# Two transformer blocks in one kernel: reciprocal sums turned on TensorE, wide projection slices, early bias rows, gate beside up

## The chip, the cores and the metric

The kernel runs on one core of a Trainium2 chip. The metric is the device time of one execution in microseconds (us), as the median of several executions. Engines are named as the profile names them: PE (TensorE), PEld (its weight loads), DVE (VectorE), ACT (ScalarE), POOL (GpSimd), SP (SyncE, which issues most DMAs).

## The reference, cut to what matters

1024 tokens of width 1024 run through two blocks, all in float32. Only the parts that the change touches are shown.

```python
# block 1: one input projection, three attentions, then a feed-forward part
proj = rmsnorm(x, attn_pre_norm) @ w_in      # 512 q + 128 k + 128 v (window attention),
                                             # 768 + 4 (forget attention), 256 + 128 + 32 (latent attention)
bias = rel_bias[t5_causal_bucket(dist)]      # window attention: 32 buckets x 8 heads, over 256 keys per row
s = q @ k.T * 64**-0.5 + bias; s = where(in_band, s, -1e30)

# block 2: window attention over 8 blocks of 128 rows, 8 heads in 2 groups, one sink per head
p = softmax(concat([sink, s_ctx, s_loc]))    # 256 context keys, up to 384 local keys
out = p_ctx @ v_ctx + p_loc @ v_loc

# block 2: 16 experts, each takes its top 128 tokens
y = (silu(xs @ w_gate) * (xs @ w_up)) @ w_down * g   # all three weights 1024 x 1024 per expert
```

## The kernel before

Float32 products run as three matmuls each (`mm3`, lines 185 to 188: high x high, high x low, low x high) on operands that `split` (lines 169 to 171) has cut in a high part (ACT) and a low part (DVE). A planner orders each engine's instructions ahead of time from the program's order and its own estimate of readiness; the engines then run their lists in that order and wait on semaphores. SP's list is one such queue: a DMA issue that waits holds up those behind it.

**Opening of block 1.** `x_load` loads one of eight tiles of 128 tokens, normalizes it and transposes it on PE (`to_T`). `slice_mm` multiplies a tile with a slice of the token-major columns of the projection. These 804 columns are cut in four slices `SL` of 196, 204, 204 and 200 columns; the first runs inside the loop over `x`, the other three after `feat_proj`, from tiles `wht`, `wlt` of a pool of their own (`a2`). `feat_proj` (line 262) makes five groups of 128 columns the other way round, 512 tokens at a time. Between them the relative bias is made: one matmul (line 330) gives 8 rows of 384 values on 8 partitions, and one DMA (line 333) writes each of them 128 times to the DRAM tensor `toep_d`, from which `toep` is read back skewed (line 342) for the window attention.

**Attention of block 2.** Steps are counted by u = 8 t + h. `att_scores` makes one head's scores, their minimum on DVE (line 1128) and the exponential with its sum on ACT (line 1132). `att_pT` transposes four heads' probabilities of one key block on PE (line 1159) and copies them out on ACT or DVE; `att_pv` multiplies them with the values (line 1179). One step of `ATT` says which of these follow which scores. The product is accumulated transposed, in one PSUM tile `po` for a block t, and there is one such buffer (`PSO = 1`), so the next block's product begins when DVE has read `po` (line 1183). Each column of `po` is a query, so the reciprocal sums, which come as [query, head], are needed along the columns: line 1142 writes `rec` to DRAM, and line 1146 reads it back twice, spread over 64 partitions each. Meanwhile POOL scales and splits the output weights `wor`, which SP loads in the same queue.

**Experts.** For each of 16 experts and four groups of 256 hidden columns, `ex_gu` multiplies 128 gathered tokens with a gate tile and an up tile, each of 1 MB ([128, 8 x 256]), 48 matmuls of 256 columns into the two halves of `pg`; `ex_T` turns the result; `ex_down` multiplies it with a third tile of 1 MB, 12 matmuls of 512 columns. Weight tiles are fetched in the order of `order` into a ring of 17 buffers, and `wsplit` splits each in two pieces of 1024 columns (lines 1487, 1488). `x_T` transposes the next expert's tokens at the end of an expert.

Of the kernel before, what the change touches and what calls it, by code (L numbers as in the profile page):

```python
# [17 lines left out]
P = 128  # L18
S = 1024
# [73 lines left out]
def tile_two_blocks(ctx, tc, A, out):  # L93
# [50 lines left out]
    rec_d = [dram.tile([8, P], F32, name=f"rec_d{t}") for t in range(NT)]  # L144
# [78 lines left out]
    swa_pool = AP_(name="swa", bufs=1, side="left")  # L223
    qa = swa_pool.tile([P, 8, S], F32R, name="qa")
    kad = swa_pool.tile([P, 2, S], F32R, name="kad")
    kal = swa_pool.tile([P, 2, S], F32R, name="kal")
    va = swa_pool.tile([P, NT, P], F32, name="va")
# [32 lines left out]
    blank_lo(kal, 2)  # L260

    def feat_proj(f, done):
# [5 lines left out]
        for hf in range(2):  # L268
# [11 lines left out]
    def slice_w(pool, c0, w, nk=8):  # L280
        wh = pool.tile([P, 8, 204], F32R, name="wht", tag="wht")
        wl = pool.tile([P, 8, 204], F32R, name="wlt", tag="wlt")
        for k in range(0, 8, nk):
            raw = pool.tile([P, nk, 204], F32, name="rawt", tag="rawt", bufs=1)
            nc.sync.dma_start(raw[:, :, :w], A["w1t"].rearrange("p (k c) -> p k c", k=8)[:, k:k + nk, c0:c0 + w])
            split(wh[:, k:k + nk, :w], wl[:, k:k + nk, :w], raw[:, :, :w])
        return wh, wl

    def slice_mm(t, wh, wl, w, parts):
        ps = ps_o.tile([P, 512], F32, name="ps", tag="po")  # L290
        for k in range(8):
            mm3(ps[:, :w], hT_hi[:, k, trow(t)], hT_lo[:, k, trow(t)], wh[:, k, :w], wl[:, k, :w], k == 0, k == 7)
        for (dst, s0, s1, d0) in parts:
            nc.scalar.copy(dst[:, t, d0:d0 + s1 - s0], ps[:, s0:s1])

    with TP(name="a0", bufs=1, side="right") as a0:
        g1 = row_in(a0, "attn_pre_norm")
        swt = []

        def x_load(t, _):  # L300
# [11 lines left out]
        def x_mm(t, _):  # L312
            slice_mm(t, swt[0][0], swt[0][1], SL[0][1], SL[0][2])

# [7 lines left out]

    with TP(name="a5", bufs=1, side="right") as a5:
        rb = a5.tile([33, 8], F32, name="rb")
        nc.vector.memset(rb, -BIG)
        nc.sync.dma_start(rb[0:32, :], A["rel_bias"])
        oh = a5.tile([33, 384], F32, name="oh")
        nc.sync.dma_start(oh, A["onehot"])
        psB = ps_s.tile([P, 1024], F32, name="psB", tag="s")
        nc.tensor.matmul(psB[0:8, :384], rb, oh, start=True, stop=True)  # L330
        rowb = a5.tile([8, 384], F32, name="rowb")
# [8 lines left out]
    tp_pool = AP_(name="toep", bufs=1, side="right")  # L340
    toep = tp_pool.tile([P, 8, 256], F32, name="toep")
    nc.sync.dma_start(toep, toep_d[:, 127:127 + 383 * P].rearrange("h (p m) -> p h m", m=383)[:, :, 0:256])
# [762 lines left out]
    def att_scores(t, h, pb=None):  # L1105
# [28 lines left out]
        if h == 7:  # L1134
# [29 lines left out]
    def att_pv(g, c):  # L1164
# [10 lines left out]
        b = h // 4  # L1175
        for i in range(nk):
# [4 lines left out]
        if h + G == 8 and j == len(vt) - 1:  # L1181
            rb = atts[t][4]
            nc.vector.tensor_tensor(out=rb, in0=po, in1=rb, op=ALU.mult)
# [269 lines left out]
    for i in range(4 * NE + 2):  # L1453
        if i < 4 * NE:
            order += [("w_gate", i), ("w_up2", i)]
        if i >= 2:
            order.append(("w_down2", i - 2))
# [42 lines left out]
    with TP(name="sel", bufs=1, side="left") as sel, TP(name="selp", bufs=2, space=PSUM) as pst:  # L1500
# [22 lines left out]
        for wname, i in (("w_gate", 0), ("w_up2", 0)):  # L1523
# [81 lines left out]
    with TP(name="exg", bufs=2, space=PSUM) as psg, \  # L1605
# [40 lines left out]
        def ex_gu(i, _):  # L1646
# [16 lines left out]
            for gi, wname in enumerate(("w_gate", "w_up2")):  # L1663
# [212 lines left out]
```

## Time and profile before

| what | before |
|---|---|
| median of 3 executions | 2552.72 us (2550.89 to 2553.92) |
| the profiled execution | 2561.14 us, of which the span of its instructions is 2559.3 us |
| mean granted TensorE clock in it | 0.964 |
| PE busy | 2363.4 us, 92% of the span, 14750 matmuls |
| DVE, ACT, POOL busy | 63%, 44%, 22% |
| DMA | 384.04 MB, mean 150 GB/s |

A line of waits reads: engine, tile and line that waited, who released it, total us, times, longest. A line of the timeline reads: start, duration, engine, line, operation, out<-in, and in brackets the idle time before it and what ended it. Matmuls are pipelined: a matmul's cost in a stream is the distance between two starts, which is shorter than its duration.

### The profile page before, as it was taken

How to read it: one execution, taken by the hardware profiler on the slowest of the kernel's cores; microseconds unless marked ns; L12 is line 12 of the kernel's file. 1: busy time of each engine (PE TensorE's matmuls, PEld its weight loads, DVE VectorE, ACT ScalarE, POOL GpSimd, SP SyncE). 2: the span in 40 equal slices, each digit the busy share in tenths (PEclk: the TensorE clock that was granted, in tenths of full speed). 3: DMA queues.
4: the chain of work that ended last, by engine and by line, in shares of the span. 5: the costliest groups of instructions: out<-in, count | busy, mean ns of one | idle time of the engine just before them, and what ended most of it. 6: DMA issues, size and time to landing. Idle time of an engine off the chain costs nothing. (4 is left out here: it accounts for less than half of the span.)

```text
span 2559.3 us, 37811 instructions
## 1 busy us (share of the span) xinstructions
PE 2363.4 (92%) x14750; PEld 1982.4 (77%) x14750; DVE 1618.4 (63%) x2572; ACT 1116.0 (44%) x1940; POOL 570.6 (22%) x596
## 2 busy tenths in 40 slices
PE   7599999999999999999997999887958999999996
PEld 7497777787887878788877988554747999989885
DVE  4217557456677665444568733564377999988886
ACT  4217357443331222222224312432135778777775
POOL 1000252131000000000016200343053554464412
PEclk9799999999999999999999999889978999999998
DMA  4400103234243332111135110112787999999975
GB/s 142 91 21 31 51 18 96 79 115 141 95 148 108 116 99 66 41 50 50 52 89 149 59 50 13 33 43 81 256 299 291 370 373 383 384 362 347 352 253 206
DMA packets 126287, 384.04 MB, mean 150 GB/s; under 512 B 21183, under 2 KB 34432, under 8 KB 109724
## 3 DMA queue, kind: packets, MB, share of 16 engines
q1 hardware_dynamic: 114444, 347.54, 38.6%
q0 software_dynamic: 6048, 22.02, 3.7%
q10 hardware_dynamic: 5616, 12.06, 1.2%
q8 instruction: 116, 1.90, 0.3%
q14 instruction: 63, 0.52, 0.1%
HBM read 342.17 MB, written 39.40 MB: 149 GB/s over the span
## 5 line engine op out<-in xcount | busy, mean ns | idle before, releaser
L1488 DVE TENSOR_TENSOR wl<-raw,wh 128x1024 fp32r<-128x1024 f32 x378 | 469.6, 1274 | 58.7 <-ACT wh L1487 55.5
L1487 ACT CAST wh<-raw 128x1024 fp32r<-128x1024 f32 x382 | 392.5, 1050 | 89.3 <-PE pg L188 62.8
L186 PE MATMUL pg<-wh,xh 128*128 128x256 f32 x1024 | 295.3, 288 | 4.5 <-ACT xh L170 4.5
L187 PE MATMUL pg<-wl,xh 128*128 128x256 f32 x1024 | 294.5, 288 | 0.0
L188 PE MATMUL pg<-wh,xl 128*128 128x256 f32 x1024 | 293.0, 286 | 0.0
L186 PE MATMUL psu<-hT_hi,wh 128*128 128x512 f32 x704 | 278.7, 396 | 7.2 <-ACT wh L170 7.1
L170 ACT CAST wh<-raw 128x512 fp32r<-128x512 f32 (+1 forms) x177 | 107.4, 641 | 404.9 <-PE psu L187 230.4
L187 PE MATMUL psu<-hT_lo,wh 128*128 128x512 f32 x704 | 278.1, 395 | 0.0
L188 PE MATMUL psu<-hT_hi,wl 128*128 128x512 f32 x704 | 277.2, 395 | 0.2 <-DVE wl L171 0.2
L163 POOL TENSOR_TENSOR rrstd<-vrstd,neghalf 128x1 f32<-128x1 f32 x51 | 34.3, 700 | 849.5 <-DVE vrstd L160 849.4
L171 DVE TENSOR_TENSOR wl<-raw,wh 128x512 fp32r<-128x512 f32 (+1 forms) x177 | 124.6, 732 | 147.8 <-ACT wh L170 147.3
L869 DVE TENSOR_TENSOR ffn_y<-ffn_y,psd 128x512 f32<-128x512 f32 x160 | 108.6, 685 | 157.7 <-PE psd L188 157.1
L186 PEld LDWEIGHTS pg<-wh,xh 128*128 128x128 f32 x1024 | 198.2, 194 | 8.5 <-ACT xh L170 6.1
L188 PEld LDWEIGHTS pg<-wh,xl 128*128 128x128 f32 x1024 | 198.1, 193 | 3.2
L187 PEld LDWEIGHTS pg<-wl,xh 128*128 128x128 f32 x1024 | 198.2, 194 | 2.4 <-DVE wl L1488 0.3
L1621 POOL TENSOR_SCALAR hot<-iota,slot 128x128 bf16<-128x128 f32 x112 | 181.1, 1636 | 25.4 <-PE pi L1629 25.4
L186 PEld LDWEIGHTS psu<-hT_hi,wh 128*128 128x128 f32 x704 | 133.2, 189 | 39.4 <-ACT wh L170 9.4
L188 PEld LDWEIGHTS psu<-hT_hi,wl 128*128 128x128 f32 x704 | 133.0, 189 | 31.4 <-DVE wl L171 1.1
L187 PEld LDWEIGHTS psu<-hT_lo,wh 128*128 128x128 f32 x704 | 133.3, 189 | 30.1
L186 PE MATMUL psd<-wh,acth 128*128 128x512 f32 x352 | 140.0, 398 | 2.6 <-DVE ffn_y L869 2.4
L187 PE MATMUL psd<-wl,acth 128*128 128x512 f32 x352 | 139.1, 395 | 0.0
L188 PE MATMUL psd<-wh,actl 128*128 128x512 f32 x352 | 138.1, 395 | 0.0
(484 smaller groups left out, 5551.7 us busy)
## 6 DMA issues: line engine op xcount, KB each, us to landing
raw<-in_w_gate SPq DMA_DIRECT2D x64, 1024.0 KB
raw<-in_w_up SPq DMA_DIRECT2D x64, 1024.0 KB
raw<-in_w_down SPq DMA_DIRECT2D x64, 1024.0 KB
wa<-in_w_ada SPq DMA_DIRECT2D x48, 512.0 KB
raw<-in_w_up SPq DMA_DIRECT2D x88, 256.0 KB
raw<-in_w_down SPq DMA_DIRECT2D x44, 256.0 KB
raw<-in_w2t SPq DMA_DIRECT2D x36, 256.0 KB
xt<-in_x SPq DMA_DIRECT2D x16, 512.0 KB
```

The costliest lines, as they stand in the source:

```text
L163: nc.gpsimd.tensor_tensor(out=r, in0=v, in1=neghalf[:, :n], op=ALU.pow)
L170: nc.scalar.copy(hi, src)
L171: nc.vector.tensor_tensor(out=lo, in0=src, in1=hi.bitcast(F32), op=ALU.subtract)
L186: nc.tensor.matmul(ps, lh, rh, start=start, stop=False)
L187: nc.tensor.matmul(ps, lh, rl, start=False, stop=False)
L188: return nc.tensor.matmul(ps, ll, rh, start=False, stop=stop)
L869: nc.vector.tensor_tensor(out=yt, in0=yt, in1=ps, op=ALU.add)
L1487: nc.scalar.copy(wh, raw[:, sl])
L1488: (eng or nc.vector).tensor_tensor(out=wl, in0=raw[:, sl], in1=wh.bitcast(F32), op=ALU.subtract)
L1621: nc.gpsimd.tensor_scalar(hot[:, t, :], iota1, slot_of[e][:, t, :], None, op0=ALU.is_equal)
```

## The change

Four parts. (1) In block 2's attention `rec` is no longer written to DRAM: ACT copies it with each value repeated 64 times ([128, 8, 64]), PE transposes that in four 128 x 128 pieces into a PSUM tile `psR` just before the last products of a block, ACT copies `psR` to `rc`, and DVE multiplies `po` with `rc`. (2) The 804 columns are cut in two slices of 388 and 416, both multiplied in the loop over `x`; their weights come in chunks of two k (2 x 388 or 2 x 416 columns) with two raw buffers. (3) The bias is made before that loop: each head's bucket column is spread over 128 columns, so that eight matmuls give 128 equal rows on 128 partitions, evacuated to four tiles `rep`, and four DMAs (at the loop's fourth tile) write `toep_d`; `toep` is read back after the first `feat_proj`. (4) Gate and up weights lie interleaved: a tile of 1 MB holds 4 of the 8 k with 256 gate and 256 up columns each, and 24 matmuls of 512 columns fill all of `pg`. Pools are moved accordingly (`va` to the pool of `vf`; `qa`, `kad`, `kal` and `toep` after the loop over `x`).

```diff
-    with TP(name="a5", bufs=1, side="right") as a5:
-        nc.tensor.matmul(psB[0:8, :384], rb, oh, start=True, stop=True)
-        nc.scalar.activation(rowb, psB[0:8, :384], AF.Copy, scale=-1.0)
-        nc.sync.dma_start(toep_d.rearrange("h (p m) -> h p m", m=384), rowb.unsqueeze(1).to_broadcast([8, P, 384]))
+    nc.vector.tensor_scalar(rbx, rb.unsqueeze(2).to_broadcast([33, 8, P]), -1.0, None, op0=ALU.mult)
+    for u in range(4):
+        psB = ps_s.tile([P, 2, 512], F32, name="psB", tag="s")
+        for i in range(2):
+            nc.tensor.matmul(psB[:, i, 0:384], rbx[:, 2 * u + i, :], oh, start=True, stop=True)
+        reps.append(a1.tile([P, 2, 384], F32, name="rep", tag=("wh", "wl")[u // 2]))
+        evac(reps[u], psB[:, :, 0:384])
+    def write_bias():
+        for u in range(4):
+            nc.sync.dma_start(toep_d.rearrange("h (p m) -> p h m", m=384)[:, 2 * u:2 * u + 2, :], reps[u])
...
-    SL = ((0, 196, ((va, 0, 128, 0), (vf, 128, 196, 0))),
-          (196, 204, ((vf, 0, 188, 68), (flog, 188, 192, 0), (lat, 192, 204, 0))),
-          (400, 204, ((lat, 0, 204, 12),)),
-          (604, 200, ((lat, 0, 200, 216),)))
+    SL = ((0, 388, ((va, 0, 128, 0), (vf, 128, 384, 0), (flog, 384, 388, 0))),
+          (388, 416, ((lat, 0, 416, 0),)))
...
         def x_load(t, _):
-            if t == 0:
-                swt.append(slice_w(a0, SL[0][0], SL[0][1]))
+            if t < 2:
+                slice_w(t)
+            if t == 3:
+                write_bias()
...
     for f in range(4):
         feat_proj(f, lambda ps, c, f=f: q_evac(ps, qa, f, f + 4, c, -0.125))
+        if f == 0:
+            nc.sync.dma_start(toep, toep_d[:, 127:127 + 383 * P].rearrange("h (p m) -> p h m", m=383)[:, :, 0:256])
-    with TP(name="a2", bufs=2, side="right") as a2:
-        for (c0, w, parts) in SL[1:]:
-            wh, wl = slice_w(a2, c0, w, 2)
-            for t in range(NT):
-                slice_mm(t, wh, wl, w, parts)
...
-            nc.sync.dma_start(rec_d[t].rearrange("h q -> q h"), rec)
-            rb = ab.tile([P, 4, P], F32, name="rb", tag="rb", bufs=2)
-            for i in range(2):
-                row = rec_d[t].rearrange("(k i) q -> i k q", i=2)[i:i + 1].partition_broadcast(64)
-                nc.sync.dma_start(rb[64 * i:64 * i + 64], row.rearrange("p o k q -> p (o k) q"))
+            rb = ab.tile([P, 8, 64], F32, name="rb", tag="rb", bufs=2)
+            nc.scalar.copy(rb, rec.unsqueeze(2).to_broadcast([P, 8, 64]))
...
+        if last:
+            psR = ps_t.tile([P, 4, P], F32, name="psR", tag="tp")
+            for u in range(4):
+                nc.tensor.transpose(psR[:, u, :], rb[:, 2 * u:2 * u + 2, :].rearrange("p i n -> p (i n)"), ident)
+            rc = ab.tile([P, 4, P], F32, name="rc", tag="rc", bufs=1)
+            nc.scalar.copy(rc, psR)
...
-            nc.vector.tensor_tensor(out=rb, in0=po, in1=rb, op=ALU.mult)
+            nc.vector.tensor_tensor(out=rb, in0=po, in1=rc, op=ALU.mult)
...
-            for gi, wname in enumerate(("w_gate", "w_up2")):
-                w = ahead.pop((wname, i), None) or wsplit(wload(wname, i))
-                o = pg[:, gi * 256:gi * 256 + 256]
-                for k in range(8):
-                    mm3(o, xh[:, k, :], xl[:, k, :], *part(w, k * 256, 256), k == 0, k == 7)
+            for hf in range(2):
+                w = ahead.pop(("w_gu", 2 * i + hf), None) or wsplit(wload("w_gu", 2 * i + hf))
+                for kk in range(4):
+                    k = 4 * hf + kk
+                    mm3(pg, xh[:, k, :], xl[:, k, :], *part(w, kk * 512, 512), k == 0, k == 7)
```

## Rows read from the trace of the kernel before

**Rows 1.** Windows of the opening: PE, PEld, DVE, ACT, POOL busy; clock; DMA share; GB/s.

```profile
0.00:50.00 50.00, 36.42 (x271) 34.82 (x272) 25.54 (x43) 25.42 (x54) 6.97 (x16) 1.00 0.53 169
50.00:100.00 50.00, 23.01 (x90) 17.72 (x89) 7.66 (x11) 7.66 (x12) 0.00 (x0) 0.73 0.46 80
...
150.00:200.00 50.00, 48.92 (x434) 48.43 (x433) 4.37 (x19) 9.80 (x31) 0.71 (x2) 1.00 0.06 16
```

**Rows 2.** Waits from 40 to 130 us, all engines.

```profile
ACT wht L170 <- DMA rawt<-in_w1t: 40.1, 6, 28.9
...
PE ps L186 <- DVE qa L175: 27.0, 1, 27.0
```

**Rows 3.** Timeline of SP's queue in the opening: DMA issues.

```profile
54.30 0.83 SPq L333 DMA_DIRECT2D toep_d<-rowb  x1
...
88.64 0.37 SPq L342 DMA_DIRECT2D toep<-toep_d x1
```

**Rows 4.** Timeline of PE: bias, 512 columns after the gap, 384 columns.

```profile
52.95 0.81 PE L330 MATMUL psB<-oh,rb 33*8 33x384 f32 x2
...
95.15 0.63 PE L186 MATMUL ps<-hT_hi,wh 128*128 128x512 f32 x1
95.58 0.63 PE L187 MATMUL ps<-hT_lo,wh 128*128 128x512 f32 x1
...
379.01 0.35 PE L186 MATMUL pq<-wqh,cth 128*128 128x384 f32 x1
379.19 0.34 PE L187 MATMUL pq<-wql,cth 128*128 128x384 f32 x1
```

**Rows 5.** Waits in block 2's attention, 1590 to 1790 us.

```profile
PE po L1179 <- DVE rb L1183: 25.9, 7, 6.4
```

**Rows 6.** Window inside that attention, columns as in the first group.

```profile
1660.00:1680.00 20.00, 16.63 (x97) 10.18 (x96) 11.60 (x20) 7.51 (x18) 11.66 (x16) 0.83 0.22 48
```

**Rows 7.** The chain of waits through that attention: start, us, what.

```profile
1628.81 9.56 DMA rec_d<-rec
...
1642.50 0.70 DVE rb L1183
...
1651.79 10.33 DMA rec_d<-rec
...
1769.05 9.65 DMA rec_d<-rec
...
1781.80 8.07 DMA xh<-x_d
```

**Rows 8.** Timeline of PE and ACT: one step of that attention.

```profile
1655.66 0.42 PE L415 MATMUL psS<-kd,q 128*128 128x384 f32 x1
...
1656.00 0.59 ACT L236 COPY pt<-psP 128x512 f32<-128x512 f32 x1 [1.39 <-PE psP L1159]
...
1656.55 0.65 PE L1179 MATMUL po<-pt,v 128*64 128x256 f32 x4
...
1657.13 0.66 PE L1159 MATMUL psP<-ident,pb 128*128 128x128 f32 x4
...
1657.55 0.42 PE L415 MATMUL psS<-kd,q 128*128 128x384 f32 x1
```

**Rows 9.** Timeline of PE in the experts: down (512 columns), gate and up (256).

```profile
2055.60 0.39 PE L187 MATMUL py<-wl,ah 128*128 128x512 f32 x1
...
2057.92 0.39 PE L188 MATMUL py<-wh,al 128*128 128x512 f32 x1
...
2060.15 0.28 PE L186 MATMUL pg<-wh,xh 128*128 128x256 f32 x1
...
2062.55 0.28 PE L188 MATMUL pg<-wh,xl 128*128 128x256 f32 x1
```

**Rows 10.** Windows in the experts, columns as in the first group.

```profile
2000.00:2050.00 50.00, 50.00 (x359) 46.69 (x358) 46.31 (x51) 39.67 (x51) 22.05 (x16) 1.00 1.00 389
...
2300.00:2350.00 50.00, 48.23 (x347) 45.00 (x347) 43.08 (x45) 37.66 (x46) 20.86 (x12) 0.99 0.98 340
```

**Rows 11.** The chain of waits after an expert's boundary late in the stage.

```profile
2298.25 0.21 PE pg L187
```

More of the change, by code (lines that the diff above doesn't have):

```diff
@@ L143, in tile_two_blocks @@
     f_d = dram.tile([4, S], F32, name="f_d")
-    rec_d = [dram.tile([8, P], F32, name=f"rec_d{t}") for t in range(NT)]
     def trow(t):
@@ L222, in tile_two_blocks @@
     fcum = vf_pool.tile([P, NT, 4], F32, name="fcum")
[L223 to L227, printed above, removed]
+    va = vf_pool.tile([P, NT, P], F32, name="va")
     ps_t = AP_(name="ps_t", bufs=2, space=PSUM, side="right")
@@ L259, in tile_two_blocks @@
     a1 = AP_(name="a1", bufs=2, side="right")
-    blank_lo(kal, 2)
     def feat_proj(f, done):
@@ L273, in feat_proj @@
             done(ps, c)
-    SL = ((0, 196, ((va, 0, 128, 0), (vf, 128, 196, 0))),
-          (196, 204, ((vf, 0, 188, 68), (flog, 188, 192, 0), (lat, 192, 204, 0))),
-          (400, 204, ((lat, 0, 204, 12),)),
-          (604, 200, ((lat, 0, 200, 216),)))
[L280 to L290, printed above, removed]
-        for k in range(8):
-            mm3(ps[:, :w], hT_hi[:, k, trow(t)], hT_lo[:, k, trow(t)], wh[:, k, :w], wl[:, k, :w], k == 0, k == 7)
-        for (dst, s0, s1, d0) in parts:
-            nc.scalar.copy(dst[:, t, d0:d0 + s1 - s0], ps[:, s0:s1])
+    rb = a1.tile([33, 8], F32, name="rb", bufs=1)
+    nc.vector.memset(rb, -BIG)
+    nc.sync.dma_start(rb[0:32, :], A["rel_bias"])
+    oh = a1.tile([33, 384], F32, name="oh", tag="raw", bufs=2)
+    nc.sync.dma_start(oh, A["onehot"])
+    rbx = a1.tile([33, 8, P], F32, name="rbx", tag="raw", bufs=2)
+    nc.vector.tensor_scalar(rbx, rb.unsqueeze(2).to_broadcast([33, 8, P]), -1.0, None, op0=ALU.mult)
+    reps = []
+    for u in range(4):
[9 more added lines that the diff above has]
+          (388, 416, ((lat, 0, 416, 0),)))
     with TP(name="a0", bufs=1, side="right") as a0:
@@ L298, in tile_two_blocks, with slice_w @@
         swt = []
+        def slice_w(j):
+            c0, w, _ = SL[j]
+            wh = a0.tile([P, 8, w], F32R, name=f"wht{j}")
+            wl = a0.tile([P, 8, w], F32R, name=f"wlt{j}")
+            for k in range(0, 8, 2):
+                raw = a0.tile([P, 2, 416], F32, name="rawt", tag="rawt", bufs=2)
+                nc.sync.dma_start(raw[:, :, :w], A["w1t"].rearrange("p (k c) -> p k c", k=8)[:, k:k + 2, c0:c0 + w])
+                split(wh[:, k:k + 2, :], wl[:, k:k + 2, :], raw[:, :, :w])
+            swt.append((wh, wl))
         def x_load(t, _):
@@ L312, in x_mm @@
         def x_mm(t, _):
-            slice_mm(t, swt[0][0], swt[0][1], SL[0][1], SL[0][2])
+            for j, (c0, w, parts) in enumerate(SL):
+                wh, wl = swt[j]
+                ps = ps_o.tile([P, 512], F32, name="ps", tag="po")
+                for k in range(8):
+                    mm3(ps[:, :w], hT_hi[:, k, trow(t)], hT_lo[:, k, trow(t)], wh[:, k, :], wl[:, k, :], k == 0, k == 7)
+                for (dst, s0, s1, d0) in parts:
+                    nc.scalar.copy(dst[:, t, d0:d0 + s1 - s0], ps[:, s0:s1])
         pipelined(NT, x_load, x_mm)
@@ L1175, in att_pv @@
         b = h // 4
+        last = h + G == 8 and 4 // G * c + nk == len(vt)
+        if last:
+            rb = atts[t][4]
+            psR = ps_t.tile([P, 4, P], F32, name="psR", tag="tp")
[3 more added lines that the diff above has]
+            nc.scalar.copy(rc, psR)
         for i in range(nk):
@@ L1180, in att_pv @@
                                  pt[:, i, hh], start=j == 0, stop=j == len(vt) - 1)
-        if h + G == 8 and j == len(vt) - 1:
-            rb = atts[t][4]
-            nc.vector.tensor_tensor(out=rb, in0=po, in1=rb, op=ALU.mult)
+        if last:
+            rb = rb.rearrange("p (u i) n -> p u (i n)", i=2)
+            nc.vector.tensor_tensor(out=rb, in0=po, in1=rc, op=ALU.mult)
             for u in range(2):
@@ L1454, in tile_two_blocks @@
         if i < 4 * NE:
-            order += [("w_gate", i), ("w_up2", i)]
+            order += [("w_gu", 2 * i), ("w_gu", 2 * i + 1)]
         if i >= 2:
@@ L1522, in tile_two_blocks @@
                 src = rest
-        for wname, i in (("w_gate", 0), ("w_up2", 0)):
+        for wname, i in (("w_gu", 0), ("w_gu", 1)):
             with tc.issue_after(W["h"].ins):
@@ L1815, in lay @@
     L["wrouter"] = kp(i["w_router_2"][0]).reshape(P, -1)
-    def ew(w):
-        return w.reshape(NE, 8, P, 4, 256).transpose(0, 3, 2, 1, 4).reshape(NE * 4, P, 2048)
-    L["w_gate"] = ew(i["w_gate_2"][0])
-    L["w_up2"] = ew(i["w_up_2"][0])
+    gu = np.stack([i["w_gate_2"][0].reshape(NE, 2, 4, P, 4, 256), i["w_up_2"][0].reshape(NE, 2, 4, P, 4, 256)], 5)
+    L["w_gu"] = gu.transpose(0, 4, 1, 3, 2, 5, 6).reshape(NE * 8, P, 2048)
     L["w_down2"] = i["w_down_2"][0].reshape(NE * D, D)
```

18 lines of the change are left out of this document (7 added, 11 removed).

## The prediction

> **What bounds the kernel now.** I read the page's busy shares first (PE 92%), then windows of 50 us through the whole span, to find the stages in which PE is not full. Three bear on the change. In the opening PE has 36.42 us of work in the first 50 us, 23.01 in the second, and from 150 us on it is full [rows 1]. The waits of that stretch say why: PE stood still once for 27.0 us, put down to DVE's reading of a projection's PSUM tile, while ACT waited 28.9 us in one piece for the raw weights of the second slice [rows 2]. ACT runs in order, so its copy of `qa` stood behind that cast, DVE behind ACT, PE behind DVE. The raw weights were late because SP had issued the write of `toep_d` at 54.30 just ahead of them; `toep`, which waits for that write, could be issued only at 88.64 [rows 3]. So the write of 8 rows, 128 times each, took about 33 us and held up what shared the engines with it.
>
> In block 2's attention PE is busy for 16.63 of 20 us at a granted clock of 0.83 [rows 6]. It waited 25.9 us in seven pieces, 6.4 the longest, for DVE to read `po` [rows 5]. The chain of waits shows what DVE waited for: from `rec_d` at 1628.81 to DVE's product at 1642.50, 13.7 us, are the trip through DRAM; the next trip begins at 1651.79, a period of 23.0 us per block of 128 rows [rows 7].
>
> In the experts PE is busy all the time, with DVE at 46.31 of 50 us and the DMA engines at a share of 1.00 [rows 10]. PE sets the pace there, with the others close behind.
>
> **Opening, term by term.** *The gap goes:* the new write starts from 128 equal rows on 128 partitions, and nothing that ACT must cast stands behind it at a time when PE needs it. That gives back 27.0 us. After the gap twelve matmuls of 512 columns ran 0.43 apart [rows 4] where 0.23 is usual [rows 9]: 12 x 0.20 = 2.4 us. *Wide slices:* the four slices are 8 x 4 x 24 = 768 matmuls; in the window from 150 us they come at 48.92 / 434 = 0.113 us each [rows 1], so 86.6 us. In the new form there are 384. A matmul of 384 columns costs 0.18 [rows 4], one of 512 costs 0.232 (eleven rows, ten distances, 2055.60 to 2057.92 [rows 9]); between them I take 0.182 for 388 and 0.193 for 416, so 192 x 0.375 = 72.0 us. The gain is 14.6 us. *Bias early:* eight matmuls stand for one, at up to 0.81 us [rows 4], in front of the first token tile. PE has some 13.6 us with nothing to do in the first 50 [rows 1], but the bias's PSUM tiles are those that the first tile's sum of squares needs. Lower bound nothing; upper bound seven more at half clock, 7 x 1.62 = 11 us; I take 3. *Second slice's weights:* 3.3 MB instead of 0.8 MB must come, be cast and split before PE can run freely. At the 169 GB/s of the first 50 us [rows 1] 2.5 MB more are 15 us; the lower bound is nothing, as PE already has the first slice's products to do; I take 4. *Turn into window attention:* the late slices covered its first scores and exponentials; without them PE may wait between nothing and three steps of 1.9 us [rows 8]; I take 2. *The write itself* (four DMAs of 384 KB): even at its old 33 us it would end inside the loop over x, now some 80 us long; behind it in SP's queue are x tiles, of which three are buffered, so I cost it at nothing, with its price inside the 15 us above. Moving `va` and the pools costs no instruction. Sum: 27.0 + 2.4 + 14.6 - 3 - 4 - 2 = **35 us** less; from the bounds 13 to 44.
>
> **Attention, term by term.** One step at full clock: scores 0.89 us (1655.66 to 1656.55), four products 0.58, four transposes 0.42 [rows 8]. A block has eight heads and ten groups of the others: 8 x 0.89 + 10 x 1.00 = 17.1 us of PE. *Removed:* three DMA issues per block on SP, and the wait. *Added:* four transposes on PE, 0.42; on ACT two copies of 512 columns, 0.59 each by its copy out of PSUM [rows 8]; no DVE instruction more. *New wait:* `po` is now free about 0.59 (copy of `psR`) + 0.70 (DVE's product [rows 7]) after the last products, plus queueing behind one copy; the next block's product comes 0.89 + 0.42 later on PE. So 0 to 0.8 us per block are open; I take 0.8. Ahead of the transposes lies ACT's copy of `rec`, made six steps earlier. Six periods run from 1628.81 to 1769.05 [rows 7], 140.2 us. The new six: 6 x (17.1 + 0.4 + 0.8) = 110, plus 5 for waits on scores and DVE's slow moments that stay: 115. That gives 25. DVE (11.60 of 20) and ACT (7.51) [rows 6] have room for it. Outside the six: the first block's wait, up to the longest of 6.4 us [rows 5], and the end, where SP issues the loads `xh` of the next stage at 1781.80, behind the last trip that began at 1769.05 [rows 7]. They move up by about 12 us; PE has products of its own for half of that, so I count 6. Sum: 25 + 6 + 6 = **37 us** less. Bounds: nothing, if the new wait is as long as the old; 48, without the 5 and with all 12 at the end.
>
> Four transposes more per block are where a published rule speaks against the change. The trace first: in the step of rows 8, four transposes cost 0.42 us together, and the steps run at full clock with transposes in each. The Trainium skill, "TensorE: Matmul & The Clock Gate", Part 4, gives about 275 ns for one transpose in a kernel and holds that transposes run at the lower clock. By its figure the 32 more would be 8.8 us, an estimate, against 3.4 by the row. No wait of that size shows between the rows' transposes; what it says of the clock is a rival below.
>
> **Experts.** 48 matmuls of 256 columns become 24 of 512; weight bytes, casts and splits stay, and each piece of 1024 columns still feeds PE for 1.4 us. By rows 9 a matmul of 256 columns costs 0.120 (21 rows, 20 distances, 2060.15 to 2062.55), one of 512 costs 0.232. So 2 x 0.120 - 0.232 = 0.008 us, 1536 times: **12 us** less. DVE allows a stage up to 7% shorter, and this is 2%; DMA stands at its ceiling of 389 GB/s [rows 10], but the ring of 17 tiles is full at the start and covers 2%. What stays open is the planner's order at an expert's end. Early windows hold 359 to 375 matmuls (five, first shown), late ones 336 to 347 (four, one shown) [rows 10]; late in the stage the matmuls behind a boundary run 0.21 apart [rows 11], half clock. In sums that is 250/1829 = 0.137 against 200/1370 = 0.146 us per matmul, 6.8%, or 20 us over the half of the stage concerned. The new order may put all experts in the slow form (8 us more than now) or none (32 less); I take the mixture as it is.
>
> The isolated spacing of the same skill's page ("Back-to-back issue gap": columns over 2.4 GHz plus 2.5 ns) would make 109 and 216 ns, thus 2.6 ns per pair and 4 us in all, an estimate; the rows show 120, so the narrow matmuls pay for something beside their columns, and I go by the rows.
>
> **Sum.** 35 + 37 + 12 = 84 us. The profiled execution took 2561 us (span 2559.3); 2561 - 84 = 2477. The median of the runs is 8.4 lower, so 2552.7 - 84 = **2469 us**.
>
> **Rivals.**
> *The clock stays low in attention.* By rows 6 the granted clock is 0.83, and if the transposes and not the waits hold it there, PE's 132 us of work in that stage take 132/0.83 = 159, 27 more: 2496. The page's rule above on transposes says so; against it stands the full-clock step of rows 8. Chance 0.10.
> *Experts in the slow form throughout:* 20 us worse than forecast, 2489. For it: the half-clock rows. Against: k 0 to 3 now run first, for twice as long, before the second half of `xh` is needed. 0.12.
> *The opening gives back what it gains*, with the second slice's weights and the bias at their upper bounds: 35 becomes 13, 2491. 0.10.
> *The attention's trip was hidden:* the period stays at 23 because `po` is released as late as now by DVE's or ACT's queue: 2506. Against: DVE's 11.60 of 20 us. 0.04.
> *Other side, slower:* the transposes stop PE itself. Before, only DVE stood on the reciprocals while PE ran six steps of other work; if the planner places the four transposes right behind a block's last scores, PE and all scores behind it wait for minimum, exponential, sum, reciprocal and copy. To eat the 47 us of the other parts and the 5 us that a measurement can tell, a block must take 6.5 us more than its 23.0, so each stop must last 12 us. The copies involved are 0.59 to 0.70 long. 0.04.
> *Better than forecast,* below 2445, by the fast form in all experts: 0.08.
> The forecast itself (2445 to 2495 as its own range): 0.52.
>
> From these, leaving out no more than 2 in 10: 2435 to 2512. A measurement tells about 0.2% (5 us) from no change. Faster by more than that: every case but the slower one, less 0.01 for mixtures of the others that come out near no change, so 0.95; within: 0.01; slower: 0.04.
>
> **What would show it.** Opening: no PE gap over 5 us after the first transposes; `toep` issued long before window attention needs it; the first window-attention transposes some 35 us earlier. Attention: no wait of PE on `po` over 2 us, a period near 18 to 19 us, granted clock above 0.95, `xh` issued right after the last block. Experts: 512-column matmuls 0.23 apart, an expert 0.8 us shorter where it has the fast form. Wrong would be: a new wait of PE on `rb` or `psR`; ACT waiting for `rawt` in the loop over x; experts of 39 us from the first on.

## The result, and the profile after

| what | before | after |
|---|---|---|
| median on the same chip | 2553.32 us | 2458.29 us (2455.66 to 2460.9) |
| ratio after / before | | 0.9619, 95% interval 0.9588 to 0.965 |
| span of the profiled execution | 2559.3 us | 2458.9 us |
| mean granted TensorE clock | 0.964 | 0.977 |

95 us less, where 84 were predicted; the range of 2435 to 2512 holds the time. The spans of the two profiled executions differ by 100 us, 5 more than the medians, as that of before was longer than most. Three markers divide these 100 us. The first transposes of block 1's window attention begin at 160.2 (before 200.3); from block 2's first attention transposes to the first expert's token transposes it takes 289.5 us (before 339.7); from there to the end of the span 609 us (before 625).

**Opening.** PE's timeline, the first rows and two rows of the loop over x, then SP's issues for the bias:

```profile
5.87 10.78 PE L282 MATMUL psB<-oh,rbx 33*128 33x384 f32 x16 [5.87 <-DVE rbx L277]
18.89 1.97 PE L195 MATMUL psT<-ident,xt 128*128 128x128 f32 x8 [2.24 <-DVE vrstd L159]
...
24.24 1.12 PE L195 MATMUL psT<-ident,xt 128*128 128x128 f32 x4 [2.03 <-DVE hT_lo L170]
...
59.88 0.35 PE L185 MATMUL ps<-wht,hT_hi 128*128 128x416 f32 x1
...
64.23 0.35 PE L187 MATMUL ps<-wht,hT_lo 128*128 128x416 f32 x1
...
65.82 0.34 PE L185 MATMUL ps<-wht,hT_hi 128*128 128x388 f32 x1
66.00 0.34 PE L186 MATMUL ps<-wlt,hT_hi 128*128 128x388 f32 x1
```
```profile
17.67 0.69 SPq L288 DMA_DIRECT2D toep_d<-rep  x1
...
102.15 0.38 SPq L349 DMA_DIRECT2D toep<-toep_d  x1
```

The bias products are on PE for 10.78 us at the very start, and the first token's transposes move from 12.6 us to 18.89. One stop of 2.24 us stands ahead of these and one of 2.03 behind; the 27.0 us of [rows 2] have no counterpart, and PE's windows read 25.00 of 25 from 25 us to 125. The spacing of 416 columns is (64.23 - 59.88) / 23 = 0.189 us, that of 388 is 0.18. The last write of `toep_d` is issued at 17.67 and the read at 102.15, 58 us ahead of the first window transposes.

**Block 2's attention.** Windows of the stage, first of before, then of after, columns as in [rows 1]:

```profile
1594.00:1680.00 86.00, 71.42 (x442) 44.89 (x442) 49.96 (x97) 37.00 (x86) 32.15 (x45) 0.88 0.17 35
1680.00:1760.00 80.00, 64.99 (x411) 40.52 (x409) 52.03 (x83) 33.31 (x77) 31.68 (x43) 0.91 0.15 37
1760.00:1826.00 66.00, 56.42 (x250) 43.58 (x251) 17.40 (x31) 2.82 (x7) 9.00 (x42) 0.90 0.62 205
```
```profile
1560.00:1640.00 80.00, 77.67 (x541) 49.89 (x540) 60.59 (x114) 47.96 (x110) 42.45 (x58) 1.00 0.12 37
1640.00:1700.00 60.00, 59.48 (x411) 37.89 (x410) 41.40 (x82) 33.12 (x75) 26.36 (x39) 1.00 0.22 74
1700.00:1741.00 41.00, 41.00 (x182) 33.94 (x181) 11.51 (x16) 0.00 (x0) 5.23 (x35) 1.00 0.74 243
```

PE stood still for 232 - 192.8 = 39.2 us before and for 181 - 178.1 = 2.9 us after. The other 14.7 us are PE's own: with 32 transposes more it is busy for less time, as the granted clock is 1.00 instead of 0.88 to 0.91. The new operations, by their tile (duration in ns: shortest, median, longest), and the end of one block in the timeline:

```profile
L1180 PE MATMUL psR<-ident,rb x32: 271/273/328, 1577.9 to 1696.6; 128*128 128x128 f32 x32
L1182 ACT COPY rc<-psR x8: 575/576/585, 1578.6 to 1696.9; 128x512 f32<-128x512 f32 x8
```
```profile
1622.66 0.62 ACT L1145 COPY rb<-rec 128x512 f32<-128x512 f32 x1
...
1632.20 0.60 PE L1180 MATMUL psR<-ident,rb 128*128 128x128 f32 x4
...
1633.65 0.58 ACT L1182 COPY rc<-psR 128x512 f32<-128x512 f32 x1
...
1634.32 0.69 DVE L1190 TENSOR_TENSOR rb<-po,rc 128x512 f32<-128x512 f32 x1 [0.94 <-PE psS L418]
...
1635.06 0.65 PE L1186 MATMUL po<-pt,v 128*64 128x256 f32 x4 [0.33 <-DVE rb L1190]
```

The order is the predicted one: ACT's copy of `rec` 9.5 us ahead (five steps, where the prediction had six), transposes, copy, DVE's product, the next block's product. PE waits 0.33 us for `po` here and 0.5 us in the whole stage, where [rows 5] had 25.9. `xh` is issued from 1691.99 on, 5.6 us ahead of the last block's product; before, at 1781.80 [rows 7], it was 1.1 us ahead of it.

**Experts.** Late ones are still slower than early ones: from one expert's first token transposes to the next it is 35.43 to 35.51 us five times (before 36.22, five times), then 39.6 and 40.8 (37.65 and 42.0), then 37.7 (38.4 to 40). PE's timeline in an early expert, then at a late boundary:

```profile
1991.11 0.39 PE L187 MATMUL pg<-wh,xl 128*128 128x512 f32 x1
1991.34 0.40 PE L185 MATMUL pg<-wh,xh 128*128 128x512 f32 x1
```
```profile
2203.11 1.03 PE L195 MATMUL psT<-ident,xs 128*128 128x128 f32 x8
2204.89 0.50 PE L185 MATMUL pg<-wh,xh 128*128 128x512 f32 x1 [0.75 <-ACT xh L169]
...
2206.60 0.44 PE L1686 MATMUL pT<-ident,sg 128*128 128x128 f32 x2 [0.97 <-DVE xl L170]
```

512 columns come 0.23 apart (1991.11 to 1991.34), as the prediction had it. At a late boundary eight transposes stand together and PE stops twice, for 0.75 and 0.97 us; in the early periods it doesn't stop at all.

### The profile page after: what moved, and what is told of

It reads as the page before. It is cut to its first block, busy times and chain, and to the rows that moved or that the text cites. A ratio compares the mean times of both kernels' runs of the same rounds, so it can differ in the third digit from the quotient of the medians.

```text
span 2458.9 us, 33986 instructions
## 1 busy us (share of the span) xinstructions
PE 2327.6 (95%) x12876; PEld 1875.0 (76%) x12876; DVE 1616.6 (66%) x2570; ACT 1120.4 (46%) x1928; POOL 596.8 (24%) x596
## 5 line engine op out<-in xcount | busy, mean ns | idle before, releaser
L169 ACT CAST wh<-raw 128x512 fp32r<-128x512 f32 (+1 forms) x177 | 107.5, 641 | 413.2 <-PE psu L186 227.7
L185 PE MATMUL pg<-wh,xh 128*128 128x512 f32 x512 | 204.8, 400 | 5.2 <-ACT xh L169 5.2
L1628 POOL TENSOR_SCALAR hot<-iota,slot 128x128 bf16<-128x128 f32 x112 | 202.7, 2553 | 19.3 <-PE pi L1636 19.2
L186 PE MATMUL pg<-wl,xh 128*128 128x512 f32 x512 | 204.4, 399 | 0.2 <-DVE wl L1495 0.2
L187 PE MATMUL pg<-wh,xl 128*128 128x512 f32 x512 | 202.3, 395 | 0.0
L185 PEld LDWEIGHTS pg<-wh,xh 128*128 128x128 f32 x512 | 96.5, 189 | 25.8 <-ACT xh L169 7.1
L186 PEld LDWEIGHTS pg<-wl,xh 128*128 128x128 f32 x512 | 96.7, 189 | 24.4 <-DVE wl L1495 5.7
L187 PEld LDWEIGHTS pg<-wh,xl 128*128 128x128 f32 x512 | 96.5, 188 | 18.9
```

Of the source, the lines that this page charges most:

```text
L169: nc.scalar.copy(hi, src)
L185: nc.tensor.matmul(ps, lh, rh, start=start, stop=False)
L186: nc.tensor.matmul(ps, lh, rl, start=False, stop=False)
L187: return nc.tensor.matmul(ps, ll, rh, start=False, stop=stop)
L1628: nc.gpsimd.tensor_scalar(hot[:, t, :], iota1, slot_of[e][:, t, :], None, op0=ALU.is_equal)
```

## The experiments

In what follows a difference in us to the kernel before is 2553 x (1 - ratio), with the ratio's 95% interval carried along: the kernel before, run beside each experiment, had medians from 2553.3 to 2559.8, so ratios compare better than times. A period of attention is the distance between two blocks' products `rb` on DVE; the eight of a run give the mean.

### The parts alone

The attention part alone:

```diff
-            nc.sync.dma_start(rec_d[t].rearrange("h q -> q h"), rec)   # and the read back
+            nc.scalar.copy(rb, rec.unsqueeze(2).to_broadcast([P, 8, 64]))   # psR and rc as in after
```


> The kernel before with the turn of the reciprocals in block 2's attention alone (no DRAM trip; four transposes of rb into psR, copy rc). Theory: the trip held po and so PE for about 4 us per block and the loads of the next stage at the end; the traces of before and after put 50.8 us between the first scores of that stage and the start of the product behind it, so about 49 us less than before, 2504 us, PE at 19.6 of 20 us there and xh issued about 50 us earlier in relation to the stage's start. Rival 1: part of that came from the earlier start of the stage (what the planner put there), then 37 us less or fewer. Rival 2: half of the gain in the stage is given back in the experts, whose weights then come no earlier (the ring of weight tiles is full at its start): 25 us less, with longer expert periods than the 36.22 of before.

Measured: 2508.67 us, ratio 0.98 (0.9761 to 0.9838): 51 us less (41 to 61). The theory holds; the gain is neither the planner's nor given back in the experts, whose steady periods are 36.22 as before. `xh` is issued at 1727.45, 132 us behind the stage's first transposes, where it was 187.5 us before.

The experts' part alone:

```diff
-                order += [("w_gate", i), ("w_up2", i)]
+                order += [("w_gu", 2 * i), ("w_gu", 2 * i + 1)]   # one 512-column matmul for two of 256
```


> The kernel before with the experts' gate and up weights side by side alone (512-column matmuls, pieces of 1024 columns as before). Theory: 1536 pairs of matmuls save 0.008 us each, 12 us less; the traces of before and after put 15 us between the experts' start and the end of the span, with steady periods of 35.45 for 36.22 us, so 12 to 15 us less, 2538 to 2541 us. Rival: the experts are bound by DVE's splits or by the weights' DMA and the 15 us came from their earlier start; then less than 4 us.

Measured: 2547.32, ratio 0.9951 (0.993 to 0.9971): 12.5 us less (7 to 18); steady periods 35.42 to 35.50. The theory holds.

The opening alone (wide slices and early bias):

```diff
-    SL = (four slices; the last three after the projections; bias written from 8 rows after the loop)
+    SL = (two slices in the loop over x; bias before it, written from 128 rows)
```


> The kernel before with both edits of the opening (wide slices in the x loop, early bias rows written from 128 partitions), attention and experts as before. Theory: 40 us earlier at window attention's first transposes, as in after, of which some 6 are given back by the end of window attention: 31 to 35 us less than before, and less than the 17 of either edit alone twice over, since either alone takes most of the 27.0 us stop away. Rival: the edits add up without overlap at the end (34 to 35) or the stage gives back more (under 28).

Measured: 2525.58, ratio 0.9887 (0.9864 to 0.9909): 29 us less (23 to 35), a little under the theory's 31 to 35; the interval covers it and the rival's under 28 too. 40.2 us are there at the first window transposes (160.1). The three parts alone add up to 51 + 12.5 + 29 = 92.5 us; together they gave 2553 x (1 - 0.9619) = 97 (89 to 105). Within these intervals the parts add up.

### What the write of the bias cost

Three kernels take the opening apart. Early bias rows, with narrow slices at their old place:

```diff
+            if t == 3:
+                write_bias()          # SL, slice_w and slice_mm as before
```


> The kernel before with the bias rows written early from 128 equal rows, and toep read after the first projection, but with the four narrow slices where they were. Theory: the 27.0 us stop of PE goes and with it 2.4 us of cold restart; the eight bias products in front of the first token tile cost 6 us (the first transposes moved by 6.3 us in after): 23 us less, 2530 us, and no stop of PE over 5 us after the first transposes. Rival: the stop is that of the second slice's raw weights themselves, which come 2.5 us apart at a time when DMA is loaded with x and other weights, and not of the write ahead of them: then ACT waits for rawt as long as before and the time is 2553 us or, with the 6 us, 2559.

Wide slices, with the bias written as before:

```diff
+    SL = ((0, 388, ...), (388, 416, ...))    # the a5 block (rowb, one DMA) and toep's read as before
```


> The kernel before with the two wide slices in the x loop, and the bias block (8 rows, each written 128 times by one DMA) and the read of toep where they were. Theory: the slices save 14.6 us of PE, and the raw weights that stood behind the write are gone from its shadow; the write now holds only the raw weights of the projections and then toep, which the window attention needs. With the write at 33 us and the read behind it, PE stops in front of the first bias addition for 0 to 15 us: 15 to 40 us less than before, 2513 to 2538. Rival: what is held is whatever comes next behind the write, the raw weights of the next projection now: the stop of about 27 us stays, at another tile, and the time is 2538 us or, with a toep later than the attention needs, more.

The write from 128 rows, at its old place:

```diff
-        nc.sync.dma_start(toep_d..., rowb.unsqueeze(1).to_broadcast([8, P, 384]))
+            evac(rep, psB[:, :, 0:384])       # for u in 0..3: two heads' 128 equal rows
+            nc.sync.dma_start(toep_d...[:, 2 * u:2 * u + 2, :], rep)
```


> The kernel before; only the bias block differs: the products give 128 equal rows, and four DMAs write them from 128 partitions, at the same place in SP's queue as the one DMA from 8 rows. Theory: the form of the write is slow (34.3 us from its issue to that of the read behind it in before, 34.6 in slices_only, where next to nothing else was moving); from 128 partitions the 1.5 MB take 6 to 10 us, the second slice's raw weights come that much earlier, PE's stop of 27.0 us falls to 0 to 8: 19 to 27 us less than before, less 3 us for seven more products in the middle of the stage. Rival: the pieces of 1536 bytes at the DRAM end set the time, then the write takes 34 us as before and the time is that of before plus 3.

Measured: bias_only 2542.46, ratio 0.9932 (0.9912 to 0.9951), 17 us less (12 to 22), where 23 were expected: 23.9 us are there at the first window transposes (176.5) and some of it is lost behind them. slices_only 2542.83, 0.9931 (0.9909 to 0.9953), 18 less (12 to 23), which fits the theory's 15 to 40 and the 15 of its rival as well. The trace is nearer to the rival: the stop is there at another tile, at 14.2 us, half of the 27.0. rows128 2536.53, 0.9926 (0.9902 to 0.9949), 19 less (13 to 25), as expected. SP's timeline of slices_only, ACT's longest wait in it, then SP's timeline of rows128:

```profile
104.28 0.83 SPq L327 DMA_DIRECT2D toep_d<-rowb  x1
138.84 0.40 SPq L341 DMA_DIRECT2D toep<-toep_d  x1
139.33 8.92 SPq L259 DMA_DIRECT2D raw<-in_w1f  x3
```
```profile
145.59 1.04 ACT L170 CAST wh<-raw 128x1024 fp32r<-128x1024 f32 x1 [18.57 <-DMA raw<-in_w1f]
```
```profile
55.34 7.48 SPq L337 DMA_DIRECT2D toep_d<-rep  x3
...
64.77 0.36 SPq L337 DMA_DIRECT2D toep_d<-rep  x1
68.05 0.36 SPq L346 DMA_DIRECT2D toep<-toep_d  x1
```

The read can be issued when the write has landed. From 8 rows that is 34.6 us after its issue, with no other DMA issued by SP in between; from 128 rows it is 12.7 us from the first of the four issues, and PE's 27.0 us stop is gone without any change of place. With the slow write and other work behind it (slices_only) ACT stands 18.57 us for the next raw weights, now a projection's, and PE 14.2. There the read of `toep` stood ahead of them in SP's list, and they were issued right behind it, at 139.33. So the form of the write is the cause; whatever comes next in SP's queue pays for it. From 110 to 130 us of slices_only, with only the write under way, the DMA engines were busy 0.46 of the time and moved 48 GB/s. The two forms differ in the partitions (8 and 128) and in the number of DMAs (one and four); no run sets these apart.

### How the DRAM trip held the attention

The trip is kept, but ACT copies `po` out at once, so that the next block's products need not wait for the reciprocals:

```diff
+            pc = ab.tile([P, 4, P], F32, name="pc", tag="pc", bufs=1)
+            nc.scalar.copy(pc, po)
-            nc.vector.tensor_tensor(out=rb, in0=po, in1=rb, op=ALU.mult)
+            nc.vector.tensor_tensor(out=rb, in0=pc, in1=rb, op=ALU.mult)
```


> The kernel before with the DRAM trip kept, but ACT copies po out to pc as soon as it is complete, so that the next block's products need not wait for the trip. Theory: what PE waited for was po alone; then the period per block falls from 23.0 to 18 to 19 us as in after (25 to 31 us less), and only the end keeps a wait for the last trip: 30 to 38 us of the 50.3 that att_only took from this stage. Rival: the trip itself, with its DMA issues on SP among the loads of weights, sets the period, or the low granted clock comes from something else: 0 to 8 us less.

Measured: 2537.76, ratio 0.9931 (0.9909 to 0.9952): 18 us less (12 to 23), a miss: half of the 30 to 38. The period is 19.7 (before 23.3, after 16.8). Two lines of its waits, then one stop in its timeline:

```profile
DVE rb L1185 <- DMA rb<-rec_d: 24.6, 6, 10.3
...
PE psS L415 <- ACT pb L1132: 15.4, 9, 6.1
```
```profile
1616.16 0.69 DVE L1185 TENSOR_TENSOR rb<-pc,rb 128x512 f32<-128x512 f32 x1 [6.43 <-DMA rb<-rec_d]
...
1618.41 0.79 ACT L1132 ACTIVATE pb<-psS,nm 128x640 f32<-128x640 f32 x1 [7.58 <-DVE nm L1129]
...
1619.35 0.69 PE L415 MATMUL psS<-kd,q 128*128 128x384 f32 x1 [6.15 <-ACT pb L1132]
```

DVE runs in order: while its product waits for the trip, the minima of the next heads' scores (`nm`) stand behind it, then ACT's exponentials, then PE's next scores, whose PSUM tile those exponentials still have to read. PE's waits of this kind are 15.4 us here and were 6.4 before. The trip reached PE on two paths, through `po` and through DVE's list; freeing `po` closes one. Taking the trip away closes both, and the wait for the last trip at the stage's end (10.3 us here).

The prediction's slower rival, brought about by emitting the turn behind a block's last reciprocal and not ahead of its last products:

```diff
             atts[t].append(rb)
+            psR = ...; four transposes of rb; rc = ...; nc.scalar.copy(rc, psR)   # moved here from att_pv
```


> The kernel after with the turn of the reciprocals (psR, rc) emitted behind a block's last reciprocal and not ahead of its last products. Theory: psR then stands on PE one or two steps behind the last scores, the chain of minimum, exponential, sum, reciprocal and copy is some 4 to 5 us long, so PE waits 1 to 3 us in each of eight blocks: 8 to 20 us slower than after. Rival: the order still leaves enough work in front (and DVE, ACT are ahead by then): within 3 us of after.

Measured: 2503.52, ratio 0.9792 (0.9769 to 0.9814): 44 us slower than after, more than twice what was expected. A line of its waits, and one stop:

```profile
PE psR L1149 <- ACT rb L1145: 32.6, 8, 5.1
```
```profile
1661.54 1.23 DVE L1138 TENSOR_TENSOR sk<-nm,small 128x8 f32<-128x8 f32 x1
...
1663.47 0.20 DVE L1142 RECIPROCAL rec<-rec 128x8 f32<-128x8 f32 x1
...
1663.77 0.62 ACT L1145 COPY rb<-rec 128x512 f32<-128x512 f32 x1 [0.76 <-DVE rec L1142]
...
1664.44 0.66 PE L1149 MATMUL psR<-ident,rb 128*128 128x128 f32 x4 [4.54 <-ACT rb L1145]
```

PE stands from the last scores until `sk`, the reciprocal and ACT's copy are through: 4.54 us here, 4.1 per block on average. The period is 22.9, so a stop costs 6.1. The other 2 us are PE's own time: from the stage's first transposes to the last block's product the same 938 matmuls keep PE busy for 150.4 us at a granted clock of 0.91, and for 134.6 us at 1.00 in after. The same instructions some five steps earlier in PE's list give back nearly all that the removed trip had brought.

### Width of the experts' matmuls

```diff
-                    mm3(pg, xh[:, k, :], xl[:, k, :], *part(w, kk * 512, 512), k == 0, k == 7)
+                    # 22 of the 24 matmuls of 512 columns as two of 256
```


> The kernel after, in the experts with 22 of the 24 matmuls of 512 columns per piece as two of 256 (first and last stay wide). Layout, loads, casts and splits are those of after. Theory: the width of the matmul is what saved time: 1408 pairs by 0.008 us, 11 us slower than after, steady periods of 36.2 us as in before, 2469 us. Rival: what saved time is the order of the work (both halves of k for gate and up together, hence fewer waits on the weights' splits), or DVE bounds both: within 3 us of after.

Measured: 2469.53 beside 2458.29 of after, 11 us more; the ratios' intervals overlap (0.9605 to 0.9698 against 0.9588 to 0.965), but the steady period is 36.21, that of before to 0.01 us. Two rows of its timeline, each of two matmuls of 256:

```profile
2025.04 0.40 PE L1679 MATMUL pg<-wh,xh 128*128 128x256 f32 x2
2025.28 0.40 PE L1679 MATMUL pg<-wl,xh 128*128 128x256 f32 x2
```

A pair takes 0.24 where one of 512 takes 0.23. In steady experts the width alone makes the gain. Over the whole stage it doesn't: from the first expert's token transposes to the end of the span it takes 625 us before, 618 in gu_narrow and 609 in after. So 9 us are the width's; of the other 7, the 128 pairs that stay wide explain 1. These 7 are in the late experts: the first seven periods take 242 us in both (235 in after). One late period of each, before, gu_narrow, after:

```profile
2334.04:2372.50 38.46, 36.69 (x266) 34.00 (x265) 34.01 (x37) 28.93 (x35) 20.54 (x12) 1.00 0.98 360
```
```profile
2248.80:2287.01 38.21, 36.71 (x257) 33.58 (x256) 34.00 (x37) 28.93 (x35) 20.41 (x12) 1.00 0.97 355
```
```profile
2240.81:2278.50 37.69, 35.96 (x170) 28.52 (x168) 33.88 (x37) 28.86 (x35) 21.39 (x12) 1.00 0.97 367
```

PE's busy time falls by 0.7 with the width, as in steady experts. But PE stands 1.77 us in a late period of before, 1.50 in gu_narrow and 1.73 in after; and three late periods of before had a granted clock of 0.96 and took 39.6 to 40 us, while none of gu_narrow or after fell below 1.00. That is layout or order, not width. In att_only, with the old layout too, only one late period was at 0.96 and the stage took 623 us, so what this part is worth varies between executions.

### Three attempts to go below after

Bias products in fp32r, in high and low parts:

```diff
-            nc.tensor.matmul(psB[:, i, 0:384], rbx[:, 2 * u + i, :], oh, start=True, stop=True)
+            nc.tensor.matmul(psB[:, i, 0:384], rbh[:, 2 * u + i, :], ohr, start=True, stop=False)
+            nc.tensor.matmul(psB[:, i, 0:384], rbl[:, 2 * u + i, :], ohr, start=False, stop=True)
```


> The kernel after with the bias products as two fp32r products each (high and low part of rel_bias, the one-hot rows are exact), so that the eight products at the start take about 3 to 6 us in place of 10.8. Theory: those products stand in front of the first token tile (its transposes start at 18.9 us in after, 12.6 in before) and their end sets the stage: 5 us less, 2453 us. Rival: the x loop is held by the raw weights of the two slices, so that an earlier first tile only waits longer later: within 1.5 us of after.

Measured: 2458.52, ratio 0.9621 (0.9575 to 0.9667): no change that can be told, as the rival said. The products end about 4 us earlier, and PE's first transposes wait for the token tile:

```profile
11.85 0.52 PE L288 MATMUL psB<-ohr,rbl 33*128 33x384 f32 x1
16.85 1.97 PE L195 MATMUL psT<-ident,xt 128*128 128x128 f32 x8 [4.49 <-DVE xt L325]
```

Two buffers for the experts' transposed rows, and the transposes one piece earlier:

```diff
-            xh = ex.tile([P, 8, P], F32R, name="xh", tag="xh", bufs=1)     # and xl
+            xh = exm.tile([P, 8, P], F32R, name="xh", tag="xh", bufs=2)    # and xl; MORE = 1
-            if c4 == 3 and e + 1 < NE:
+            if c4 == 2 and e + 1 < NE:
```


> The kernel after; in the experts the transposed rows xh and xl have two buffers (one weight tile fewer in the ring for it) and the next expert's transposes stand behind the third piece of gate and up, not the fourth. Theory: the slow form of late experts (37.7 us against 35.45) is PE's stop at an expert's boundary: from the eighth expert on all eight transposes stand together with the products that need xh right behind them, and PE waits 2.1 us; with the fourth piece's products in between it has work: late experts 35.5 to 36.2, so 12 to 18 us less than after, about 2444 us. Rival: DMA at a share of 0.98 is the bound of late experts and the boundary's stops only show slack: within 3 us of after, or slower by the missing weight tile.

The transposes in two halves that the program sets apart:

```diff
+                if hf == 0 and c4 == 3 and e + 1 < NE:
+                    x_T(e + 1)                          # features 0 to 511
+                if hf == 0 and c4 == 0 and e > 0:
+                    x_half(half[e], xh, xl, 1)          # features 512 to 1023
```


> The kernel after; in the experts the next expert's rows are transposed in two halves that the program itself sets apart: features 0 to 511 behind the first half of the fourth gate-and-up piece, features 512 to 1023 behind the first half of the next expert's first piece; one xh and one xl for all experts, ring and buffers as in after. Theory: late experts are slower because all eight transposes stand together there, with the products that need them right behind (stops of 0.75 and 0.97 us and more at a boundary); in halves a boundary keeps one shorter stop: late periods 36.0 to 36.8 in place of 37.7, 8 to 14 us less than after, about 2447 us. Rival: the boundary is not what makes late experts slower (as the miss of xh2c may say): late periods stay at 37.5 to 38.2, within 4 us of after.

Measured: xh2c 2479.36, ratio 0.9708 (0.9684 to 0.9732), 21 us slower than after, with periods of 37.8 to 43.6 from the third expert to the seventh and 38.2 later; halves 2464.22, 0.9631 (0.9601 to 0.9662), not to be told from after, with late periods of 38.3 to 39.6 and one of 35.45 at the end. Both theories fell. In halves the stops at a late boundary stay, as the first half stands right ahead of its products again:

```profile
2241.31 0.60 PE L1662 MATMUL psT<-ident,xs 128*128 128x128 f32 x4
...
2243.10 0.50 PE L185 MATMUL pg<-wh,xh 128*128 128x512 f32 x1 [0.97 <-ACT xh L169]
...
2244.79 0.50 PE L187 MATMUL pg<-wh,xl 128*128 128x512 f32 x1 [0.96 <-DVE xl L170]
...
2246.10 0.63 PE L185 MATMUL pg<-wh,xh 128*128 128x512 f32 x1
2246.52 0.63 PE L186 MATMUL pg<-wl,xh 128*128 128x512 f32 x1
```

In xh2c eight transposes stand together at a late boundary too, with stops of 0.75 and 0.64 us behind them. So neither an earlier emission nor a split one moved the copies out of the boundary, and xh2c changed three things at once (buffers, ring, place), so that its loss can't be put down to one of them. PE's stops make up 1.7 of the 2.2 us by which a late period of after is longer than a steady one; no run has taken them away, so why they arise only in late experts stays open.

## Why the prediction came out right, point by point

The 84 us were 11 less than the medians show. An opening put 6 us too high and an attention put 14 too low partly cancel in that sum, which is luck; the parts are judged one by one here.

**Opening, 35 predicted, 29 measured (23 to 35).** Its terms, as far as the trace of after shows them: the gap went, as said, and rows128 shows that the form of the write made it. Wide slices: 192 x (0.18 + 0.189) = 70.8 us, 15.8 less than 86.6 where 14.6 stood. The bias products were under-sized: 18.9 - 12.6 = 6.3 us, not 3, inside the bound of 11. The second slice's weights: at most one stop of 2.03, not 4; it waited for DVE's split of a token tile, behind a split of slice weights and the next tile's normalization. One sign of being wrong did show, in small: ACT waited for `rawt` in the loop, 5.6 us in five pieces, 2.6 the longest. The turn into window attention: one stop of 1.6 us, not 2. These make 29.4 + 15.8 - 6.3 - 2.0 - 1.6 = 35.3; the trace has 40.1 at that place, 4.8 of it unassigned. The new write was costed at nothing, and no stop of PE is put down to it. For what comes behind that place the prediction had no term: from there to block 2's first attention transposes it takes 1393.9 us before and 1400.0 after, so 6 us are given back. Over all runs this stretch takes 1390.7 to 1401.9 us, most of them with nothing changed in it; which order or clock makes the spread was not found.

**Attention, 37 predicted, 51 measured (41 to 61).** The mechanism held and the size was off. Six periods between DVE's products fell from 142.7 to 107.5 us, 35 where 25 stood; the first block's product came 19.8 instead of 25.7 us behind the stage's start, 5.9 (6 predicted); the last period fell from 20.2 to 10.1, 10 for the end (6 predicted, 12 the upper bound). The mis-sized step is "the new six": 110 + 5. PE's work of 6 x 17.5 = 105 was near (107.0 us busy), but the 0.8 us of new wait per block, 4.8 in all, and the 5 us of "waits on scores and DVE's slow moments that stay" together came to 0.6. The old six add 2.5: counted between products they are 142.7, not 140.2. The prediction named the wait on `po` alone; the second path, through DVE's list, is what trip_po_out shows. With the trip gone DVE no longer stalled its own minima, and PE ran at a granted clock of 1.00.

**The clock.** The rival of a low clock, 2496 us, is refuted: four more transposes per block, and the granted clock is 1.00 in every window of the stage. The Trainium skill, "TensorE: Matmul & The Clock Gate", Part 4, gives about 275 ns for one transpose; the record's duration of 273 ns agrees, but four of them together lasted 0.60 us from the first start to the last end, so the price of one more in the stream is (0.60 - 0.27) / 3 = 0.11. That a stage with more transposes runs at the lower clock, no run here shows: where the clock was low (before, rc_early), PE had been waiting.

**Experts, 12 predicted, 12.5 measured (7 to 18).** 96 pairs per expert by 0.008 us are 0.77, and 36.22 - 35.45 is 0.77. The mixture of steady and slow experts stayed, as assumed. But the profiles have 16 us between the marks, and gu_narrow leaves 9 of them to the width (11 by the medians); the rest came in the late experts, for which the prediction had no term beyond the 0.77. The Trainium skill, "TensorE: Matmul & The Clock Gate", section "Back-to-back issue gap", would make 4 us of the width, an estimate from its isolated spacing; gu_narrow's 9 to 11 us are on the side of the rows.

**The slower rival** had the right mechanism, a place in PE's list, and was absent only because the transposes stand some 9 us behind ACT's copy of `rec` (0.67 us behind it in rc_early). It asked for stops of 12 us per block to undo the whole change; rc_early's cost of 6.1 per block undoes most of the attention part.

**Slips in its sums.** The opening's rival puts the second slice's weights and the bias at their upper bounds: that leaves 35 - 11 - 8 = 16, not 13, and 2488 us. With the turn at its bound too, the lower bound is 12, not 13. The slow write took 34.3 us from its issue to that of the read [rows 3], not 33. The 132 us of PE's work in the low-clock rival come from no row; eight blocks of 17.1 are 137. The 2.6 ns per pair are 2.5. None of these moves the forecast by 1 us.

## What to carry to other kernels

When an engine that runs in order waits for a late operand, price everything behind it in its list as well as the buffer that it holds: freeing the buffer alone gave 18 of 51 us here. Look at the form of a DMA before its place: a broadcast from 8 partitions took 34 us, from 128 partitions and in four DMAs it took under 13, and other work behind the slow one changed who waits and how long (PE 14.2 us in place of 27.0) but left a wait. And emit work that depends on a long chain late: the same four transposes cost next to nothing 9 us on, and 5.5 us a block (44 us in all) right behind their source.

## What the runs showed of the hardware that was not expected

Short stops can cost more than their length. In halves two stops of 0.97 and 0.96 us within 3 us were followed by 3.5 us in which 512 columns came 0.43 apart, at a granted clock of 0.51 (the 1.2 GHz level); in after two stops of 0.75 and 0.97 at the same place left the clock at 1.00. The first of these stretches, then the one behind the stops in after:

```profile
2245.50:2249.00 3.50, 3.50 (x12) 2.61 (x11) 1.23 (x1) 1.15 (x2) 2.50 (x2) 0.51 1.07 389
```
```profile
2208.00:2213.00 5.00, 5.00 (x24) 4.10 (x23) 3.64 (x4) 4.06 (x5) 1.79 (x2) 1.00 1.03 274
```

What decides between the two these rows don't tell.

Eight products of 384 columns in float32 made 16 matmul records and took 10.78 us in after; sixteen in fp32r at the same place came 0.32 apart and were through in 6.3. So 384 columns in fp32r took 0.32 near the start of the span where 0.18 is usual, though the granted clock of that window (bias_r) reads 1.00. In after, 388 columns still come 0.32 apart up to 28 us and 0.18 behind, at 1.00 throughout.

```profile
6.00:16.00 10.00, 6.11 (x16) 4.69 (x16) 5.52 (x8) 5.80 (x9) 0.95 (x2) 1.00 1.01 369
```

Whether the record of the clock or something else is behind this, these rows don't tell; near the start the distances between starts are the safer measure.
